# More Strassen pairs in the down projections of a two-layer decoder trunk, with wider joins and gates in its up projections

## The chip, the cores and the metric

The kernel runs on one core of a Trainium2 chip. The metric is the device time of one execution in microseconds, given as the median of several runs. All inputs lie in HBM at the start, and the output is written back there.

The engines are named as in the profile: PE is TensorE (matmuls), PEld its weight loads, DVE is VectorE, ACT is ScalarE, POOL is GpSimd, and SP is the engine whose queue issues nearly all DMAs.

## The reference

The program is a decoder trunk of two layers on 256 tokens with 1024 features. Layer 0 mixes tokens with a chunked gated MLP, layer 1 with block-sparse attention that has a relative position bias. Each layer then applies a gated feed-forward part with a causal convolution of width 3. Every part ends in a layer norm of the scaled residual sum:

```python
def conv_ffn(x, w_up, conv_w, conv_b, w_down):
    h = x @ w_up                                  # 256x1024 @ 1024x5632
    hp = jnp.pad(h, ((0, 0), (CONV_WIDTH - 1, 0), (0, 0)))
    hc = conv_b
    for j in range(CONV_WIDTH):
        hc = hc + conv_w[j] * hp[:, j:j + S]
    g, val = jnp.split(hc, 2, axis=-1)
    return (jax.nn.gelu(g) * val) @ w_down        # 256x2816 @ 2816x1024

for i in range(DEPTH):
    y = chunked_gmlp(x, ...) if i % 2 == 0 else moba_attention(x, ...)
    x = layer_norm(DN_ALPHA * x + y, ln_mix_g[i], ln_mix_b[i])
    y = conv_ffn(x, ...)
    x = layer_norm(DN_ALPHA * x + y, ln_ffn_g[i], ln_ffn_b[i])
```

All of it is float32.

## The kernel before, in words

**Numbers as two parts.** PE multiplies in the format fp32r. To keep float32 precision, each operand is split into a high part (an ACT copy to fp32r) and a low part (DVE subtracts the high part from the original). A product of two operands is then three matmuls: high by high, high by low, low by high. The function `split` (line 331) records the copy and the subtraction. Most instructions pass through a few helpers, so the profile shows them under one line each: `mms` (L300) for matmuls, `act` (L312), `tt` (L318) and `stt` (L322) for DVE, `transposes` (L306).

**Weights.** Weights come as a stream of 1 MB chunks of 128x2048. `prep` (line 445) loads one chunk into one of two `raw` buffers and splits its two halves into `whi` and `wlo` tiles of 128x1024. There are ten of each, so five chunks are ready or in work at a time: when a chunk is spent, the one five places behind it is started. The feed-forward part has 22 up chunks (`f_up0`, `f_up1`) and 11 down chunks (`f_dn0`, `f_dn1`) per layer.

**Up stage** (`conv_up`, line 850). The features run over partitions. After a first pair of tiles that is computed by rows, ten groups follow, each with two gate tiles and two value tiles. Each of the four has a PSUM bank of 512 columns: 256 hold the products with the high token part and the high weights, 256 the rest (`cols_times`). A group is 64 matmuls, half with 512 columns and half with 256. After it, `join` (line 649) adds the two halves of each bank (an ACT copy, then a DVE addition, 256 columns each), and `gate` (line 860) does for each of the two feature tiles the convolution (ACT scale and shift, DVE scalar_tensor_tensor twice, for gate and value), the gelu, the product, and the split into `rr`, all on 256 columns. The scratch tile `ff` holds what lies between.

**Down stage** (`project_out`, line 657). Tokens run over partitions, two tiles of 128. For each of 22 k tiles the two halves of 512 output columns are accumulated in four banks. A pair of k tiles is one chunk. In a normal pair there are 2 x 2 x 2 products, 24 matmuls of 128x512. The pairs listed in `FAST` are done as a Strassen product with seven products, 21 matmuls (`unit`, line 680). Four of the seven use sums of weights (`weight_forms`, line 419) and four use sums of tokens (`token_forms`, line 432), three of them both, all made by DVE and split again by ACT and DVE. The gated tokens that a fast pair needs unsplit stay in `kept` places of `ff`. Four extra banks hold the four products that are common to several outputs; they run through all fast pairs of a stage and are put together once (`combine`, line 713). After the last pair the outputs get their layer norm.

```python
FAST = {"f_dn0": (4, 7), "f_dn1": (4, 5, 7)}
```

The numbers are those of the pairs, 0 to 10, in a stage; "unit 7" below is the fast pair 7.

**What sets the order.** Every step is recorded in a `Plan` with an estimated duration, and a list scheduler then sets the order on each engine. PE follows the order of recording, except for a few filling matmuls. ACT, DVE and SP follow due times, which come from PE's estimated line. So a step that is recorded at another place, or with another estimate, moves others. Each engine then runs its list strictly in that order. `build_bias` (line 539) makes the attention's bias table; before, it is recorded between the up and down stage of layer 0.

Of the kernel before, what the change touches and what calls it, by code (L numbers as in the profile page):

```python
# [11 lines left out]
F32 = mybir.dt.float32  # L12
# [41 lines left out]
FAST = {"f_dn0": (4, 7), "f_dn1": (4, 5, 7)}  # L54
# [175 lines left out]
def trunk_kernel(ctx: ExitStack, tc: tile.TileContext, a: dict, out: bass.AP):  # L230
# [43 lines left out]
    banks = [ps.tile([P, HALF], F32, name=f"bank{i}") for i in range(BANKS)]  # L274
# [3 lines left out]
    def bank(long=False):  # L278
        i = min((i for i in range(BANKS) if not bank_of[i][2]), key=lambda i: bank_of[i][0])
# [4 lines left out]
        return b  # L284

# [6 lines left out]
    def mms(seq, r, w, fill=False, ns=None, mixed=False):  # L292

        for o, l, x, _, _ in seq if ns is None else ():
            n = flat(x)
            ns = (ns or 0.0) + max(107.0, n / 2.4) + 2.5 if l.dtype == F32R else (218.0 if n <= P else n / 0.6 + 5)
# [74 lines left out]
    def raw_of(i):  # L371
        if is_fast(i) and stream[i][1] == FAST[stream[i][0]][-1]:
            early = place("ff", 2560, CH)
        elif i == 2:
# [7 lines left out]
    raw_held, forms, kept = {}, {}, {}  # L382
    inner = {}

    def used_up(k0, k1):

        bufs = []
        for b in inner["rr"]:
            n = Buf(b.ap[:, k0 * S:k1 * S], [Buf(None)])
            n.prev[0].ops = [o for k in range(k0, k1) for o in [b.wr[k], *b.rd.get(k, ())]]  # L390
            bufs.append(n)
        return bufs
# [26 lines left out]
    def weight_forms(i):  # L419

        rb, t = raw_held[i], place("ff", 0, 4 * HALF)
        b4, t4 = (x.ap.rearrange("p (a n) -> p a n", a=4) for x in (rb, t))
        tt(t4[:, 0:2, :], b4[:, 1:4:2, :], b4[:, 0:2, :], ALU.subtract, [(rb, [*range(6), 6, 7])], [(t, [0, 1])])
        tt(t4[:, 2, :], t4[:, 1, :], b4[:, 0, :], ALU.add, [(rb, [0, 1]), (t, [1])], [(t, [2])])
        tt(t4[:, 3, :], b4[:, 2, :], t4[:, 2, :], ALU.subtract, [(rb, [4, 5]), (t, [2])], [(t, [3])])
        h, l = used_up(0, KT) if stream[i][1] in FAST[stream[i][0]][1:-1] else xt_new()
        for o in (0, 2):
            parts, sl = [o, o + 1], slice(o * HALF, (o + 2) * HALF)
            split((h, parts, h.ap[:, sl]), (l, parts, l.ap[:, sl]), (t, parts, t.ap[:, sl]))
        forms[i] = h, l  # L430

    def token_forms(key):

        g, s = kept[key], place("ff", 2048, HALF)
        a11, a21, a12, a22 = (g.ap[:, j * P:(j + 1) * P] for j in range(4))
        s1, s3, s2, s4 = (s.ap[:, j * P:(j + 1) * P] for j in range(4))
        tt(s1, a21, a22, ALU.add, [(g, [0, 1])], [(s, [0])])
        tt(s3, a11, a21, ALU.subtract, [(g, [0])], [(s, [1])])
        tt(s2, s1, a11, ALU.subtract, [(g, [0]), (s, [0])], [(s, [2])])
        tt(s4, a12, s2, ALU.subtract, [(g, [1]), (s, [2])], [(s, [3])])  # L440
        h, l = (x.new() for x in tok_rings)
        split((h, [0], h.ap), (l, [0], l.ap), (s, range(4), s.ap))
        return h, l

    def prep(i):
        name, c = stream[i]
        if i > 1 and is_fast(i - 2):
            weight_forms(i - 2)
        raw = raw_of(i)
        if name != "a_v":  # L450
# [14 lines left out]
        chunks[i], raw_held[i] = subs, raw[0][0]  # L465
# [72 lines left out]
    def build_bias(at):  # L538
        rb, oh, parts = place("ff", at, P), place("ff", at + P, DIST), xth.new()
# [117 lines left out]
    def project_out(name, nk, at, xold, li, rows_i, wait=REST, first=None):  # L657
# [22 lines left out]
        def unit(c):  # L680
# [4 lines left out]
            th, tl = forms[where[name, c]]  # L685
            sh, sl = token_forms((name, c))
# [26 lines left out]
        def combine():  # L713
# [7 lines left out]
            tt(u.ap, m6.ap, u.ap, ALU.add, [m6, u], [u])  # L721
            tt(w.ap, m5.ap, u.ap, ALU.add, [m5, u], [w])
            tt(y.ap, m7.ap, u.ap, ALU.add, [m7, u], [y])
            stt(r0.ap[:, hi], r0.ap[:, hi], ALPHA, w.ap, ALU.mult, ALU.add, [(r0, ph), w], [(r0, ph)])
            x1 = r1.ap.rearrange("p (a n) -> p a n", a=2)
            stt(x1, x1, ALPHA, y.ap.unsqueeze(1).to_broadcast([P, 2, HALF]), ALU.mult, ALU.add, [(r1, QUART), y], [(r1, QUART)])
            tt(r1.ap[:, hi], r1.ap[:, hi], m5.ap, ALU.add, [(r1, ph), m5], [(r1, ph)])
            for b in sums:
                done_with(b, 0)

        for k, t in order:
            if k // 2 in units:
# [117 lines left out]
    def conv_up(layer, h, l):  # L850
        ah, al = place("rr", 0, FT * S), place("rr", FT * S, FT * S)
        inner["rr"] = ah, al
# [3 lines left out]
        hring = Places("ff", (3456, 3712, 3968, 4224, 6 * S, 7 * S, 8 * S, 9 * S), S)  # L856
# [3 lines left out]
        def gate(i, srcs):  # L860
            cs = []
            for j, (b, o) in enumerate(srcs):
                cw, c = cc[:, layer, j * FT + i, :], cring[j].new()
                act(c.ap, o, AF.Identity, [b, convc], [c], bias=cw[:, 3:4], scale=cw[:, 2:3], psum=i < 2)
# [3 lines left out]
            key, n = (f"f_dn{layer}", i // 2), 0  # L868
            if key[1] in FAST.get(key[0], ()):
                n = i % 2  # L870
                if not n:
                    kept[key] = place("ff", 4608 + HALF * FAST[key[0]].index(key[1]), HALF)
# [271 lines left out]
```

## Time and profile before

| what | value |
|---|---|
| median of 3 runs | 557.43 us (556.71 to 557.60) |
| span of the profiled execution | 555.0 us |
| PE busy | 547.0 us, 2968 matmuls |
| DVE busy | 498.9 us |
| ACT busy | 378.3 us |
| read from HBM | 109.52 MB |
| up stage of layer 0 | to 198.79 us |
| down stage of layer 0 | 198.79 to 253.5 us |
| up stage of layer 1 | to 489.7 us |
| down stage of layer 1 | 489.7 to 547.9 us |

The span is the time from the first to the last instruction of one profiled execution. A time of the run is somewhat longer: 2.4 us lie between the span and the median. A row of a timeline has the start in us, the length, engine, line, operation, tile written and tiles read, shapes and how many instructions of the kind follow each other. A matmul's length is modelled and overlaps its neighbour; the distance between starts is what a matmul costs.

### The profile page before, as it was taken

The numbers are of one execution on the slowest core, as the hardware profiler recorded it, in microseconds if no ns is written. First come the engines' busy times: TensorE is split into PE (matmuls) and PEld (weight loads), VectorE is DVE, ScalarE is ACT, GpSimd is POOL, SyncE is SP. The second block draws the span as 40 slices with busy tenths as digits, with TensorE's granted clock in tenths as the row PEclk, the third lists the DMA queues.
The fourth block names the chain that finished last, engine by engine and source line by source line (L and its number), as shares of the span: only waits on it lengthen the run. The fifth ranks groups of instructions, "written<-read, shape, count | busy, mean of one in ns | idle before, by whom it ended". The sixth has DMA issues, their size and how long they took to land.

```text
span 555.0 us, 8220 instructions
## 1 busy us (share of the span) xinstructions
PE 547.0 (99%) x2968; PEld 468.8 (84%) x2968; DVE 498.9 (90%) x967; ACT 378.3 (68%) x718; POOL 11.3 (2%) x17
## 2 busy tenths in 40 slices
PE   9999999999999999999999999999999999999994
PEld 6888888898988988888888888888898988988884
DVE  6889889999999999989948898889898999999997
ACT  6846586877877884645668877587767877776510
POOL 0010000000000000001000000000000000000001
PEclk9999999999999999999999999999999999999998
DMA  8996626686545524764565363416765466444602
GB/s 317 413 335 238 230 92 228 227 308 224 208 172 188 191 77 153 285 227 152 191 263 191 110 251 138 174 70 233 298 232 223 155 227 227 153 151 153 220 9 76
DMA packets 20105, 111.12 MB, mean 200 GB/s; under 512 B 2256, under 2 KB 5600, under 8 KB 7904
## 3 DMA queue, kind: packets, MB, share of 16 engines
q1 hardware_dynamic: 19488, 109.94, 54.7%
q10 hardware_dynamic: 576, 0.66, 0.3%
q8 instruction: 23, 0.38, 0.3%
q14 instruction: 18, 0.15, 0.1%
HBM read 109.52 MB, written 1.07 MB: 199 GB/s over the span
## 4 chain that ended last, share of the span: by engine, by line
PE 99%; DVE 1%; issue 0%; DVEq 0%
PE bank L300 96%; PE bank L306 2%; DVE x L322 0%; DVE stat L563 0%; DVEq L1140 0%; DVE stat L569 0%
## 5 line engine op out<-in xcount | busy, mean ns | idle before, releaser
L318 DVE TENSOR_TENSOR wlo<-raw,whi 128x1024 fp32r<-128x1024 f32 (+2 forms) x205 | 216.6, 1079 | 19.9 <-ACT whi L312 13.3
L312 ACT ACTIVATE whi<-raw 128x1024 fp32r<-128x1024 f32 (+2 forms) x205 | 185.1, 941 | 61.5 <-DMA raw<-in_f_up 22.2
L300 PE MATMUL bank<-xt,whi 128*128 128x512 f32 x832 | 195.9, 391 | 0.0
L300 PEld LDWEIGHTS bank<-xt,whi 128*128 128x128 f32 x832 | 154.2, 188 | 30.6
L300 PE MATMUL bank<-whi,rr 128*128 128x512 f32 (+1 forms) x428 | 134.1, 387 | 0.0
L300 PEld LDWEIGHTS bank<-xt,wlo 128*128 128x128 f32 x832 | 103.1, 192 | 2.1
L300 PE MATMUL bank<-xt,wlo 128*128 128x256 f32 x832 | 104.8, 284 | 0.0
L300 PEld LDWEIGHTS bank<-whi,rr 128*128 128x128 f32 x428 | 80.0, 188 | 16.2 <-issue 0.2
L300 PE MATMUL bank<-wlo,rr 128*128 128x512 f32 (+1 forms) x214 | 82.6, 386 | 0.0
L322 DVE SCALAR_TENSOR_TENSOR ff<-ff,convc 128x255 f32<-128x255 f32 (+1 forms) x160 | 70.4, 476 | 0.3 <-ACT ff L312 0.2
L312 ACT ACTIVATE ff<-bank 128x256 f32<-128x256 f32 (+2 forms) x126 | 49.3, 400 | 27.1 <-PE bank L300 19.9
L300 PE MATMUL bank<-whi,xt 128*128 128x512 f32 (+1 forms) x196 | 60.7, 390 | 0.0
L318 DVE TENSOR_TENSOR ff<-bank,ff 128x256 f32<-128x256 f32 (+1 forms) x110 | 45.5, 431 | 8.5 <-ACT ff L312 7.7
L312 ACT ACTIVATE ff<-ff,convc 128x256 f32<-128x256 f32 x80 | 45.0, 592 | 3.0 <-DVE ff L318 2.9
L300 PEld LDWEIGHTS bank<-wlo,rr 128*128 128x128 f32 x214 | 40.2, 188 | 7.9
L300 PEld LDWEIGHTS bank<-whi,xt 128*128 128x128 f32 x196 | 36.4, 188 | 8.3 <-ACT whi L312 1.2
L300 PE MATMUL bank<-wlo,xt 128*128 128x512 f32 (+1 forms) x98 | 36.4, 387 | 0.0
L312 ACT ACTIVATE ff<-bank,lncol 128x128 f32<-128x128 f32 x48 | 18.7, 459 | 17.5 <-PE bank L306 17.5
L318 DVE TENSOR_TENSOR ff<-ff 128x256 f32<-128x256 f32 (+3 forms) x74 | 30.3, 431 | 0.3 <-ACT ff L312 0.2
L312 ACT ACTIVATE ff<-ff 128x256 f32<-128x256 f32 x52 | 20.4, 411 | 11.3 <-DVE rr L318 6.8
L318 DVE TENSOR_TENSOR xt<-ff,xt 128x256 fp32r<-128x256 f32 (+3 forms) x32 | 21.8, 691 | 4.1 <-ACT xt L312 4.0
L312 ACT ACTIVATE rr<-ff 128x256 fp32r<-128x256 f32 (+3 forms) x50 | 21.3, 442 | 5.2 <-DVE ff L318 5.1
(75 smaller groups left out, 360.7 us busy)
## 6 DMA issues: line engine op xcount, KB each, us to landing
raw<-in_f_up SPq DMA_DIRECT2D x44, 1024.0 KB, 4.8
raw<-in_f_dn SPq DMA_DIRECT2D x20, 1024.0 KB, 4.8
raw<-in_b_qk SPq DMA_DIRECT2D x8, 1024.0 KB, 4.9
lnrow<-in_lnrow SPq DMA_DIRECT2D x5, 1024.0 KB, 6.6
raw<-in_a_u SPq DMA_DIRECT2D x4, 1024.0 KB, 8.4
raw<-in_a_out SPq DMA_DIRECT2D x4, 1024.0 KB, 6.0
raw<-in_b_v SPq DMA_DIRECT2D x4, 1024.0 KB, 4.7
raw<-in_b_o SPq DMA_DIRECT2D x4, 1024.0 KB, 4.9
```

Of the source, the lines that this page charges most:

```text
L300: nc.tensor.matmul(o, l, x, start=start, stop=stop, skip_group_check=mixed)
L306: nc.tensor.transpose(o, x, ident.ap)
L312: plan.op("act", ns, lambda: nc.scalar.activation(o, x, func, **kw), r, w, table=table)
L318: dve(70 + 1.04 * flat(x), lambda: nc.vector.tensor_tensor(o, x, y, op=op), r, w)
L322: lambda: nc.vector.scalar_tensor_tensor(o, x, s, y, op0=op0, op1=op1), r, w)
```

## The change

1. **`FAST`**: both down stages now have four fast pairs, 3, 5, 6 and 7. Before they had two (4, 7) and three (4, 5, 7).
2. **Weight sums**: they need a whole chunk unsplit. Before they were read from the `raw` buffer. Now `load_sums` loads a second copy of the chunk, in two halves of 0.5 MB, into those places of `ff` that the up stage uses for its gates, and the sums are made there in place. The `raw` load of a fast chunk takes only the three quarters that are split as plain weights. The form is another variant of the same algorithm, with sums where there were differences. The forms of pairs 3 and 6 go to the `xt` buffer, those of 5 and 7 to the part of `rr` that the stage has used up.
3. **When they are made**: the forms of pair 3 are recorded at the start of the down stage, those of pairs 5 and 6 behind unit 3, those of pair 7 behind unit 5. Each time the copy of the chunk two places further on in the list is loaded into the places that have come free. Token sums are three DVE instructions (256, 128, 128 columns) in place of four of 128. For pairs 3 and 5 they are made in the up stage.
4. **PSUM** is one tile of 128x4096. An up group takes banks 0 to 3 or 4 to 7. One ACT copy and one DVE addition of 128x1024 join all four banks, after the whole group.
5. **Gates**: gelu, product and split now cover both feature tiles at once, 512 columns. The convolution stays at 256.
6. **`build_bias`** is recorded ahead of the first up stage and uses other buffers.
7. The planner's estimate of a matmul goes from n/2.4 + 2.5 to n/2.4 + 8 ns.
8. **`combine`** has the signs of the new variant; its number of operations stays the same.

The core of the diff:

```diff
-FAST = {"f_dn0": (4, 7), "f_dn1": (4, 5, 7)}
+FAST = {"f_dn0": (3, 5, 6, 7), "f_dn1": (3, 5, 6, 7)}
...
-    banks = [ps.tile([P, HALF], F32, name=f"bank{i}") for i in range(BANKS)]
+    psum = ps.tile([P, BANKS * HALF], F32, name="bank")
+    banks = [psum[:, i * HALF:(i + 1) * HALF] for i in range(BANKS)]
...
+    def load_sums(name, j):
+        key = name, FAST[name][j]
+        raw_sums[key] = [place("ff", o + SUB * (j % 2), SUB) for o in (0, 5 * HALF)]
+        for n, b in enumerate(raw_sums[key]):
+            load(b.ap, a[name][key[1]][:, n * SUB:(n + 1) * SUB], [(b, range(2))])
+
+    def weight_forms(name, j):
...
+        h, l = xt_new() if j % 2 == 0 else used_up(0, KT)
+        tt(f[:, b22:b12 - 1:-5, :], f[:, b12:b12 + 1, :].to_broadcast([P, 2, HALF]),
+           f[:, b22:b11 - 1 if b11 else None:-6, :], ALU.add, [(r0, [0, 1]), (r1, [1])], [(r0, [1]), (r1, [1])])
+        tt(f[:, b11, :], f[:, b22, :], f[:, b11, :], ALU.add, [(r0, [0]), (r1, [1])], [(r0, [0])])
+        tt(f[:, b21, :], f[:, b11, :], f[:, b21, :], ALU.add, [(r0, [0]), (r1, [0])], [(r1, [0])])
+        for n, raw in ((1, r1), (0, r0)):
+            parts, sl = [2 * n, 2 * n + 1], slice(n * SUB, (n + 1) * SUB)
+            split((h, parts, h.ap[:, sl]), (l, parts, l.ap[:, sl]), (raw, [0, 1], raw.ap))
+        forms[key] = h, l
+        if j + 2 < len(FAST[name]):
+            load_sums(name, j + 2)
...
+        if is_fast(i):
+            for o, n in ((0, HALF), (SUB, SUB)):
+                load(raw[0][0].ap[:, o:o + n], a[name][c][:, o:o + n], [(raw[0][0], range(o // 256, (o + n) // 256))])
...
+        def more(c):
+            for j, after in enumerate([None, KT // 2 - 1, *units[:2]]):
+                if c == after and j < len(units):
+                    weight_forms(name, j)
...
-            tiles4 = [(bank(), *sub(name, i + j // 2, j % 2)) for j in range(4)]
-            cols_times(tiles4, h, l)
+            whole, four = four_banks()
+            cols_times([(b, *sub(name, i + j // 2, j % 2)) for j, b in enumerate(four)], h, l)
...
+            c = joined.new()
+            c3, b3 = (x.rearrange("p (a n) -> p a n", a=4) for x in (c.ap, whole))
+            act(c3, b3[:, :, S:], AF.Copy, four, [c], psum=True)
+            tt(c3, b3[:, :, :S], c3, ALU.add, [*four, c], [c])
...
+            act(g.ap, gv[0].ap, AF.Gelu_apprx_tanh, [(gv[0], both)], [(g, both)], table="gelu")
+            tt(g.ap, g.ap, gv[1].ap, ALU.mult, [(g, both), (gv[1], both)], [(g, both)])
+            at = slice(i * S, (i + 2) * S)
+            split((ah, [i, i + 1], ah.ap[:, at]), (al, [i, i + 1], al.ap[:, at]), (g, both, g.ap))
+            if key in kept and key[1] in FAST[key[0]][:2]:
+                token_forms(key)
```

Three places show how the instructions move.

First, DVE late in the up stage of layer 0, before. `ff<-bank` is a join, `ff<-ff,convc` the convolution, `wlo<-raw,whi` the low part of a weight half:

```order
L318 TENSOR_TENSOR ff<-bank_112,ff 128x256
L322 SCALAR_TENSOR_TENSOR ff<-ff,convc 128x254
L318 TENSOR_TENSOR ff<-bank_105,ff 128x256
L318 TENSOR_TENSOR wlo_75<-raw_86,whi_65 128x1024
L318 TENSOR_TENSOR ff<-bank_106,ff 128x256
L318 TENSOR_TENSOR ff<-bank_107,ff 128x256
L318 TENSOR_TENSOR wlo_76<-raw_86,whi_66 128x1024
L318 TENSOR_TENSOR ff<-ff 128x256 x2
```

The joins of a group are four, each behind its own bank, with a weight half and a convolution of the tiles before in between. The same place now:

```order
L326 TENSOR_TENSOR wlo_75<-raw_86,whi_65 128x1024
L326 TENSOR_TENSOR wlo_76<-raw_86,whi_66 128x1024
L326 TENSOR_TENSOR wlo_77<-raw_85,whi_67 128x1024
L326 TENSOR_TENSOR wlo_78<-raw_85,whi_68 128x1024
L326 TENSOR_TENSOR ff<-bank,ff 128x1024
L326 TENSOR_TENSOR ff<-ff 128x512
L326 TENSOR_TENSOR small<-ff,small 128x512
```

One join stands for four, behind the weight halves; a part of the token sums of a fast pair (`small`) has come into the up stage.

Second, DVE in the down stage of layer 0 up to the weight forms of unit 7, before. These go to `xt`, and the tokens' form to `small`:

```order
L318 TENSOR_TENSOR ff<-ff 128x1024
L318 TENSOR_TENSOR wlo_78<-ff,whi_68 128x1024
L318 TENSOR_TENSOR ff<-ff 128x512
L318 TENSOR_TENSOR wlo_79<-raw_86,whi_69 128x1024
L318 TENSOR_TENSOR wlo_80<-raw_86,whi_70 128x1024
L318 TENSOR_TENSOR ff<-ff 128x512
L318 TENSOR_TENSOR wlo_77<-ff,whi_67 128x512
L318 TENSOR_TENSOR xt_87<-ff,xt_87 128x1024 x2
```

And now, where the forms of unit 6 go to `xt` and those of unit 7 to `rr`:

```order
L326 TENSOR_TENSOR xt_87<-ff,xt_87 128x1024 x2
L326 TENSOR_TENSOR small<-ff,small 128x512
L326 TENSOR_TENSOR wlo_78<-raw_86,whi_68 128x1024
L326 TENSOR_TENSOR ff<-ff 128x2x512
L326 TENSOR_TENSOR wlo_77<-raw_86,whi_67 128x512
L326 TENSOR_TENSOR ff<-ff 128x256
L326 TENSOR_TENSOR ff<-ff 128x512
L326 TENSOR_TENSOR ff<-ff 128x128
L326 TENSOR_TENSOR wlo_80<-raw_85,whi_70 128x1024
L326 TENSOR_TENSOR ff<-ff 128x128
L326 TENSOR_TENSOR wlo_79<-raw_85,whi_69 128x1024
L326 TENSOR_TENSOR ff<-ff 128x512
```

The forms of unit 7 (`rr<-ff,rr`, twice 128x1024) follow two rows behind, after the tokens' form. The weight sums of 6 and 7 stand one after the other, between the splits of chunks 7 and 8.

Third, PE in the down stage of layer 0, the second half of pair 3 before, four products of three matmuls each:

```order
L300 MATMUL bank_105<-whi_70,rr 128x512
L300 MATMUL bank_105<-wlo_80,rr 128x512
L300 MATMUL bank_105<-whi_70,rr 128x512
L300 MATMUL bank_106<-whi_70,rr 128x512
L300 MATMUL bank_106<-wlo_80,rr 128x512
L300 MATMUL bank_106<-whi_70,rr 128x512
...
L300 MATMUL bank_108<-whi_70,rr 128x512
L300 MATMUL bank_108<-wlo_80,rr 128x512
L300 MATMUL bank_108<-whi_70,rr 128x512
```

And pair 3 now, the whole unit of 21 matmuls, with the weight forms in `xt` and the token forms in `small`:

```order
L308 MATMUL bank<-whi_70,rr 128x512
L308 MATMUL bank<-wlo_80,rr 128x512
L308 MATMUL bank<-whi_70,rr 128x512
L308 MATMUL bank<-whi_70,small 128x512
L308 MATMUL bank<-wlo_80,small 128x512
L308 MATMUL bank<-whi_70,small 128x512
L308 MATMUL bank<-whi_69,rr 128x512
L308 MATMUL bank<-wlo_79,rr 128x512
L308 MATMUL bank<-whi_69,rr 128x512
L308 MATMUL bank<-xt_87,rr 128x512 x3
L308 MATMUL bank<-xt_87,small 128x512 x9
```

Nine matmuls of a unit need no weight form; the tenth is the first that reads one.

More of the change, by code (lines that the diff above doesn't have):

```diff
@@ L273, in trunk_kernel, with bank @@
     x32a, x32b = Places("ff", (4608, 5120), HALF), Places("ff", (5632, 5888), S)
-    banks = [ps.tile([P, HALF], F32, name=f"bank{i}") for i in range(BANKS)]
+    psum = ps.tile([P, BANKS * HALF], F32, name="bank")
+    banks = [psum[:, i * HALF:(i + 1) * HALF] for i in range(BANKS)]
     bank_of = [(i - BANKS, None, False) for i in range(BANKS)]
     state = {"age": 0, "next": 0, "low": False}
-    def bank(long=False):
-        i = min((i for i in range(BANKS) if not bank_of[i][2]), key=lambda i: bank_of[i][0])
+    def bank(long=False, at=None):
+        i = min((i for i in range(BANKS) if not bank_of[i][2]), key=lambda i: bank_of[i][0]) if at is None else at
         old = bank_of[i][1]
@@ L284, in bank, with four_banks @@
         return b
+    def four_banks():
+        free = [i for i in (0, 4) if not any(x[2] for x in bank_of[i:i + 4])]
+        i = min(free, key=lambda i: max(x[0] for x in bank_of[i:i + 4]))
+        return psum[:, i * HALF:(i + 4) * HALF], [bank(at=j) for j in range(i, i + 4)]
     def done_with(b, age=None):
@@ L380, in raw_of @@
         return [(early, early.ap[:, s * SUB:(s + 1) * SUB], s * 4) for s in range(2)]
-    raw_held, forms, kept = {}, {}, {}
+    forms, kept = {}, {}
     inner = {}
     def used_up(k0, k1):
+        if "spare" in inner:
+            inner["spare"] = [Buf(b.ap, [b]) for b in inner["spare"]]
+            return inner["spare"]
         bufs = []
@@ L391, in used_up @@
             bufs.append(n)
+        inner["spare"] = bufs
         return bufs
@@ L417, in is_fast @@
         return c in FAST.get(name, ())
[L419 to L440, printed above, removed]
+    raw_sums = {}
@@ L464, in prep @@
             subs.append((hi, lo))
-        chunks[i], raw_held[i] = subs, raw[0][0]
+        chunks[i] = subs
     FINE = set()
@@ L684, in unit @@
             (b11, _), (b2, _) = ((x, None) for x in (sub(name, c, 0), sub(name, c, 1)))
-            th, tl = forms[where[name, c]]
-            sh, sl = token_forms((name, c))
+            th, tl = forms[name, c]
+            if (name, c) not in tokens:
+                token_forms((name, c))
+            sh, sl = tokens[name, c]
             def token(k, t):
@@ L736, in project_out @@
                     spent(name, k // 2)
+                    more(k // 2)
                     if k // 2 == units[-1]:
@@ L743, in project_out @@
                 spent(name, k // 2)
+                if units:
+                    more(k // 2)
         res = (None, None) if last else xt_new()
@@ L867, in gate @@
                 cs.append(c)
[L868 to L872, printed above, removed]
-                g = kept[key]
-            else:
-                g = gring.new()
-            gv, gp = g.ap[:, n * S:(n + 1) * S], (g, [n])
-            act(gv, cs[0].ap, AF.Gelu_apprx_tanh, [cs[0]], [gp], table="gelu")
-            tt(gv, gv, cs[1].ap, ALU.mult, [gp, cs[1]], [gp])
-            c = slice(0, P if g is kept.get(key) and not n else S)
-            split((ah, [i], av[:, i, c]), (al, [i], lv[:, i, c]), (g, [n], gv[:, c]))
+            g = gring.new()
+            act(g.ap, cs[0].ap, AF.Gelu_apprx_tanh, [cs[0]], [g], table="gelu")
+            tt(g.ap, g.ap, cs[1].ap, ALU.mult, [g, cs[1]], [g])
+            split((ah, [i], av[:, i, :]), (al, [i], lv[:, i, :]), (g, [0], g.ap))
         turned = []
```

71 lines of the change are left out of this document (46 added, 25 removed).

## The prediction

> **What bounds the kernel now.** I read the page first, then the chain of waits, then busy time by stage, and last the timelines of PE and DVE where the change works. From the page the span and the engines' shares, then two pieces of the chain (start, length) and what ends the second:
>
> ```profile
> span 555.0 us, 8220 instructions
> ...
> PE 547.0 (99%) x2968; PEld 468.8 (84%) x2968; DVE 498.9 (90%) x967; ACT 378.3 (68%) x718; POOL 11.3 (2%) x17
> ```
> ```profile
> 89.00 164.56 PE bank L300 x876
> ...
> 379.89 167.98 PE bank L300 x902
> 547.87 0.02 issue
> ```
>
> The chain never leaves PE from 89.00 to 253.55 and from 379.89 to 547.87, which is nearly all of both up stages and all of both down stages. So the time there is the number of matmuls times their spacing, and only fewer matmuls or a new wait can move it. DVE is at 90%. Whether it has room is read stage by stage: up stage 0, down stage 0 until its last fast pair has its weights, and the same for layer 1 (columns: stretch, its length, then busy time of PE, PEld, DVE, ACT, POOL, granted clock, DMA share, GB/s):
>
> ```profile
> 90.00:198.80 108.80, 108.80 (x632) 96.62 (x631) 103.05 (x191) 84.51 (x157) 0.00 (x0) 1.00 0.58 208
> 198.80:237.00 38.20, 38.20 (x170) 31.68 (x169) 36.78 (x64) 23.17 (x36) 0.00 (x0) 1.00 0.51 192
> 380.00:489.70 109.70, 109.70 (x636) 97.32 (x635) 103.12 (x191) 86.83 (x161) 0.00 (x0) 1.00 0.61 218
> 489.70:529.20 39.50, 39.50 (x176) 32.66 (x174) 39.30 (x70) 23.98 (x35) 0.00 (x0) 1.00 0.44 160
> ```
>
> PE is busy for the whole of each, at a granted clock of 1.00. DVE idles 5.75, 1.42, 6.58 and 0.20 us. That is nearly all the room there is for more Strassen pairs, whose forms DVE must make.
>
> **Fewer matmuls.** The timeline of PE in down stage 0, inside the fast pair 4, and its first row:
>
> ```profile
> 198.79 0.39 PE L300 MATMUL bank<-whi,rr 128*128 128x512 f32 x1
> ...
> 223.47 2.20 PE L300 MATMUL bank<-xt,small 128*128 128x512 f32 x9
> 225.51 0.39 PE L300 MATMUL bank<-whi,rr 128*128 128x512 f32 x1
> ```
>
> Nine matmuls of 128x512 take 225.51 - 223.47 = 2.04 us from start to start, 0.2267 us each. A normal pair of k tiles is 8 products of 3 matmuls, 5.44 us. A fast pair is 7 products, 4.76 us. Fast pairs go from 2 to 4 in down stage 0 and from 3 to 4 in down stage 1. That is three more, nine matmuls fewer, **2.04 us** (1.36 and 0.68). All of it is on the chain. [...]
>
> **What DVE pays for a fast pair.** Where DVE's time could end up on PE is unit 7, the last fast pair of both stages. These rows show it before the change: DVE's splits of its weight forms, then PE's matmuls that read them, first of down stage 0, then of down stage 1:
>
> ```profile
> 233.44 2.36 DVE L318 TENSOR_TENSOR xt<-ff,xt 128x1024 fp32r<-128x1024 f32 x2
> 235.71 2.36 DVE L318 TENSOR_TENSOR wlo<-raw,whi 128x1024 fp32r<-128x1024 f32 x2
> ```
> ```profile
> 238.43 0.84 PE L300 MATMUL bank<-xt,rr 128*128 128x512 f32 x3
> 239.11 2.20 PE L300 MATMUL bank<-xt,small 128*128 128x512 f32 x9
> ```
> ```profile
> 526.88 2.35 DVE L318 TENSOR_TENSOR xt<-ff,xt 128x1024 fp32r<-128x1024 f32 x2
> 529.15 4.62 DVE L318 TENSOR_TENSOR wlo<-raw,whi 128x1024 fp32r<-128x1024 f32 x4
> ```
> ```profile
> 528.44 0.84 PE L300 MATMUL bank<-xt,rr 128*128 128x512 f32 x3
> 529.12 2.26 PE L300 MATMUL bank<-xt,small 128*128 128x512 f32 x9
> 531.22 0.39 PE L300 MATMUL bank<-whi,rr 128*128 128x512 f32 x1
> ```
>
> The prices come from the groups of DVE instructions by shape (busy time, mean ns of one, idle before):
>
> ```profile
> L318 DVE TENSOR_TENSOR wlo<-raw,whi 128x1024 fp32r<-128x1024 f32 x153 | 183.3, 1217 | 16.6 <-ACT whi L312 10.1 <-PE bank L300 4.5 <-ACT ff L312 1.2
> L318 DVE TENSOR_TENSOR ff<-bank,ff 128x256 f32<-128x256 f32 x104 | 41.6, 417 | 8.4 <-ACT ff L312 7.7
> L322 DVE SCALAR_TENSOR_TENSOR ff<-ff,convc 128x255 f32<-128x255 f32 x80 | 36.7, 476 | 0.2 <-ACT ff L312 0.2
> L318 DVE TENSOR_TENSOR wlo<-raw,whi 128x512 fp32r<-128x512 f32 x50 | 32.5, 681 | 2.9 <-ACT whi L312 2.8
> L318 DVE TENSOR_TENSOR ff<-ff 128x256 f32<-128x256 f32 x44 | 17.4, 417 | 0.2 <-ACT ff L312 0.2
> L318 DVE TENSOR_TENSOR rr<-ff,rr 128x256 fp32r<-128x256 f32 x39 | 15.1, 417 | 0.0
> L318 DVE TENSOR_TENSOR xt<-ff,xt 128x1024 fp32r<-128x1024 f32 x8 | 9.4, 1218 | 0.0
> L318 DVE TENSOR_TENSOR ff<-ff 128x512 f32<-128x512 f32 x8 | 5.5, 684 | 0.1
> L318 DVE TENSOR_TENSOR ff<-ff 128x128 f32<-128x128 f32 x20 | 5.2, 282 | 0.0
> L318 DVE TENSOR_TENSOR small<-ff,small 128x512 fp32r<-128x512 f32 x5 | 3.4, 687 | 0.5 <-ACT small L312 0.5
> ```
>
> Neighbours overlap. Above, two of 1218 ns begin 2.27 us (235.71 - 233.44) ahead of the next row, 1.135 each, so in a run of instructions each costs 0.08 less than its mean: 1.135, 0.60, 0.34 and 0.20 us for 1024, 512, 256 and 128 columns. A fast pair of the new kernel has one weight sum and two splits of 1024 (3.41), two weight sums and the token split of 512 (1.80), and token sums of 256, 128 and 128 (0.74). It saves half the split of its chunk's first half (0.54). Sum 5.41 us, within 0.1 of the old form. The sum over a 128x2x512 view with a broadcast operand is in no row; I price it as 1024 columns, with half and twice that as ends (-0.6, +1.1 us a pair).
>
> **What the up stage gives back.** Four joins of 256 become one of 1024 (1.36 to 1.135), two products of 256 one of 512 (0.68 to 0.60), two splits likewise: 0.38 us a group, 3.8 us over ten groups. The eight scalar_tensor_tensor rows per group stay as they are. [...]
>
> So DVE's extra work is 2 x 5.41 - 3.8 = 7.0 us in layer 0 and 5.41 - 3.8 = 1.6 us in layer 1. It must be done before unit 7's forms are read, since the added pairs 3, 5 and 6 all lie ahead of unit 7.
>
> In stage 0 the last form ends at 235.8 and PE wants it at 239.11: 3.3 us to spare. In stage 1 it ends at about 529.2, just where PE wants it, and nine matmuls there take 2.10 us and not 2.04. Unit 7 already touches its limit in layer 1.
>
> The budget: layer 0 has 5.75 + 1.42 of idle, and 3.3 - 1.36 to spare, since PE will be 1.36 earlier. That is 9.1 us of room for 7.0 of work, 2.1 left. Layer 1 has 6.58 + 0.20 + 0 - 0.68 = 6.1 for 1.6, 4.5 left. By the order of the new kernel, DVE runs from the last group's join to unit 7's second form through 19 instructions of 1024, 15 of 512, eight of 0.40 (scalar_tensor_tensor), two of 256 and four of 128: 21.6 + 9.0 + 3.2 + 0.7 + 0.8 = 35.3 us. The join needs ACT's copy of 1024 columns out of PSUM first, about 1 us by four times the row of 256 less its overlap:
>
> ```profile
> L312 ACT ACTIVATE ff<-bank 128x256 f32<-128x256 f32 x104 | 38.7, 376 | 25.0 <-PE bank L300 19.9 <-DVE ff L322 1.6 <-ACT whi L312 0.8
> ```
>
> Started 1.3 us after the up stage's last matmul, it ends at +36.6. PE reaches that form after 3 normal pairs, unit 3, pair 4, units 5 and 6, and 12 matmuls of unit 7: 16.32 + 4.76 + 5.44 + 9.52 + 2.72 = +38.8. So 2.2 us to spare if DVE is on time and idles nowhere. Units 3, 5 and 6 have more. The cover is thin, and what lies over 2.2 us goes on PE in full.
>
> **Edits with one answer.** Second weight copies: 0.75 MB more per fast pair, 6 MB in all, on queues whose DMA share was 0.51 and 0.44 in the down stages above. A whole chunk lands in
>
> ```profile
> raw<-in_f_dn SPq DMA_DIRECT2D x20, 1024.0 KB, 4.8
> ```
>
> The copies for units 6 and 7 are sent when pairs 3 and 5 have left their buffers, some 3 us ahead of DVE's use; two halves of a chunk take between half of that row, 2.4, and all of it. I take no cost, because DVE has other splits queued there; at worst it is 1.8 us of DVE idle for each, which is rival one. The new wait, a join behind four finished banks, holds up on ACT the weight copies queued behind the PSUM copy, and on DVE the gates; both are wanted only a group, 11 us, later, and PE needs the four banks again after that long. The position bias, moved ahead of the first up stage, is one matmul either way. The combination of the sums has the same count. The tail behind 547.87 (7.1 us of the span) is the same. The new spacing in the planner's estimate only reorders.
>
> **The sum.** The profiled span is 555.0, the median 557.43: 2.4 us lie around it, and I keep them. 555.0 - 2.04 = 553.0, and 557.43 - 2.04 = **555.4 us**. A measurement of this kernel can tell 0.2%, 1.1 us, so the gain is visible only if at most 0.9 us of it is lost.
>
> **Rivals.** First, *unit 7 waits a little* (chance 0.22). Idle of the old kind stays in part: in up stages DVE waited for ACT like this (total us, times, longest; layer 0, then layer 1):
>
> ```profile
> DVE ff L318 <- ACT ff L312: 2.7, 7, 0.7
> ```
> ```profile
> DVE wlo L318 <- ACT whi L312: 4.1, 3, 2.1
> ```
>
> If about 3.5 of the 7.2 us of idle in layer 0 remain, unit 7 is 3.5 - 2.1 = 1.4 us late, and 557.43 - 2.04 + 1.4 = 556.8: no visible change. For it: the second stage already loses 0.06. Against: a DVE that is behind finds its inputs ready, and joins that wait for ACT fall from four to one a group.
>
> Second, *slower* (0.14): the join of four banks starts only when all four are done and ACT has copied 1024 columns, where before three of the four had been joined during the group. DVE then idles about as much as before in both up stages, every group. It is behind at the end of both, and units 5 to 7 wait: layer 0 loses 7.2 - 2.1 = 5.1, layer 1 6.8 - 4.5 = 2.3, and the time is 557.43 - 2.04 + 7.4 = 562.8. It turns slower than before once 2.04 is lost, so from about 4.1 us of idle left in layer 0 alone, 0.4 us a group; visibly from 5.2. For it: DVE is in order, and nothing behind the join can pass it. Against: there are four weight splits of 1.135 us per group, and the order has one to four of them right ahead of each join. [...]
>
> Third, *the change doesn't remove matmuls, or gives the 2 us back elsewhere*, as in a LayerNorm stage that now waits (0.04): 557.4.
>
> **How the numbers follow.** No visible stall (0.60): 555.0 to 556.3. Rival one: 556.3 to 557.6. Rival two from 558.5 to 562.8. The range that leaves out most of rival two and the odd low run (medians scatter by 0.4) is 554.9 to 557.5. Faster by over 0.2%: 0.60 and a part of rival one, 0.65. Within: 0.20. Slower: 0.15.
>
> **What would show it.** Nine fewer 128x512 matmuls and a span near 553.0, PE busy throughout 198 to 253 and the last stage, with DVE idle in the up stages down to some 2 us per layer: right. Idle before the first `xt` or `rr` weight matmul of unit 7: rival one. DVE idle of 5 us in the up stages and PE waiting in units 5, 6 and 7: rival two. A PE wait within an up group would break the view that banks come free in time.

## The result, and the profile after

The change makes the kernel slower. The median after is 563.19 us (six runs, 562.29 to 569.39), beside 557.57 for the kernel before on the same chip (556.71 to 557.73): a ratio of 1.0128, 95% interval 1.0085 to 1.0171. The forecast was 555.4, in 554.9 to 557.5. The runs after also scatter over 7 us, those of before over 1.

From the page of after, the span and the engines' shares:

```profile
span 567.7 us, 8102 instructions
...
PE 553.3 (97%) x2959; PEld 470.8 (83%) x2959; DVE 509.2 (90%) x891; ACT 374.8 (66%) x627; POOL 11.8 (2%) x17
```

The matmuls are 2968 - 2959 = 9 fewer, as announced. But PE now idles 567.7 - 553.3 = 14.4 us, where before it idled 8.0. (This is the profile of the run at 569.39, the slowest of the six.) The critical path, which was PE throughout both down stages, now has this in it, by engine and by line:

```profile
PE 78%; DVE 9%; DMA 8%; issue 3%; ACT 2%; SPq 0%; DVEq 0%; ACTq 0%
PE bank L308 75%; DMA ff<-in_f_dn 5%; DVE ff L326 4%; PE bank L314 2%; DMA raw<-in_f_dn 2%; DVE wlo L326 2%; DVE ff L330 1%; DVE rr L326 1%; ACT whi L320 1%; DMA raw<-in_head 1%; ACT xt L320 0%; DVE x L330 0%; DVE xt L326 0%; ACT rr L320 0%; DVE small L326 0%
```

`ff<-in_f_dn` is the second weight copies: 5% of the span waits for them to land. By stage, the same four stretches as before (stretch, length, busy time of PE, PEld, DVE, ACT, POOL, granted clock, DMA share, GB/s):

```profile
93.60:202.40 108.80, 108.80 (x632) 96.57 (x631) 106.42 (x165) 82.65 (x114) 0.00 (x0) 1.00 0.58 215
202.40:240.60 38.20, 37.23 (x165) 30.50 (x163) 33.67 (x47) 19.64 (x25) 0.00 (x0) 1.00 0.65 214
387.10:496.80 109.70, 109.70 (x635) 97.31 (x634) 107.12 (x165) 85.37 (x119) 0.00 (x0) 1.00 0.60 215
496.80:536.30 39.50, 36.66 (x162) 30.03 (x160) 33.76 (x47) 19.75 (x25) 0.00 (x0) 0.99 0.61 206
```

The up stages are as long as before, PE never stops in them, and DVE idles 2.4 and 2.6 us there. In the down stages DVE idles 38.20 - 33.67 = 4.5 and 39.50 - 33.76 = 5.7 us, where it idled 1.4 and 0.2, and the DMA share went from 0.51 and 0.44 to 0.65 and 0.61. What DVE waits for stands in the waits (total us, times, longest):

```profile
DVE ff L326 <- DMA ff<-in_f_dn: 8.4, 7, 2.5
```

How that reaches PE is read in the last down stage. First the chain of waits (start, length):

```profile
511.15 7.00 DMA ff<-in_f_dn
...
518.25 3.25 DVE ff L326 x5
...
524.98 5.04 DMA ff<-in_f_dn
...
530.11 1.23 DVE ff L326
...
535.55 0.60 DVE ff L326
536.15 0.61 DVE rr L326
...
536.81 8.38 PE bank L308 x24
```

Halves of the chunks land 7.00 and 5.04 us after they are sent, and PE stands at the end. DVE's own rows for that stretch, with its idle time in brackets:

```profile
510.40 0.68 DVE L326 TENSOR_TENSOR rr<-ff,rr 128x512 fp32r<-128x512 f32 x1
...
514.52 1.23 DVE L326 TENSOR_TENSOR ff<-ff 128x1024 f32<-128x1024 f32 x1 [1.10 <-DMA ff<-in_f_dn]
518.25 4.04 DVE L326 TENSOR_TENSOR ff<-ff 128x1024 f32<-128x1024 f32 x7 [2.50 <-DMA ff<-in_f_dn]
...
530.11 1.23 DVE L326 TENSOR_TENSOR ff<-ff 128x1024 f32<-128x1024 f32 x1 [1.15 <-DMA ff<-in_f_dn]
```

DVE stands at the first weight sums of units 6, 5 and 7, in this order, 4.75 us in all. Everything behind those rows in its list is late by that, the plain splits too, which need no copy. The longest wait, 2.50 us, is for the second half of unit 5's copy: it goes into a place of the up stage's gates and could be sent, at 511.15, only when DVE had split the last of them (the row at 510.40). PE's rows at the first product of unit 7, in the same stage:

```profile
532.85 0.39 PE L308 MATMUL bank<-whi,rr 128*128 128x512 f32 x1
533.08 0.39 PE L308 MATMUL bank<-wlo,rr 128*128 128x512 f32 x1
536.81 0.80 PE L308 MATMUL bank<-whi,rr 128*128 128x512 f32 x1 [3.35 <-DVE rr L326]
...
538.68 0.63 PE L308 MATMUL bank<-whi,rr 128*128 128x512 f32 x1
539.11 0.63 PE L308 MATMUL bank<-wlo,rr 128*128 128x512 f32 x1
...
543.89 0.39 PE L308 MATMUL bank<-whi,rr 128*128 128x512 f32 x1
544.12 0.39 PE L308 MATMUL bank<-wlo,rr 128*128 128x512 f32 x1
```

PE waits 3.35 us, not yet for a weight form but for the low part of unit 7's tokens, which DVE makes just ahead of the forms. After it the matmuls start 0.43 us apart (538.68, 539.11), until they are 0.23 apart again at 543.89. The first down stage has the same spacing, after two shorter waits:

```profile
240.24 0.50 PE L308 MATMUL bank<-whi,small 128*128 128x512 f32 x1 [0.97 <-ACT small L320]
...
241.85 0.61 PE L308 MATMUL bank<-whi,small 128*128 128x512 f32 x1 [0.89 <-DVE small L326]
242.25 0.63 PE L308 MATMUL bank<-whi,rr 128*128 128x512 f32 x1
242.68 0.63 PE L308 MATMUL bank<-wlo,rr 128*128 128x512 f32 x1
```

In these two stretches the granted clock is 0.50, and 1.00 between them:

```profile
242.10:245.50 3.40, 3.40 (x8) 2.20 (x8) 3.40 (x4) 2.73 (x5) 0.00 (x0) 0.50 0.73 289
245.50:535.65 290.15, 287.96 (x1610) 245.44 (x1608) 260.70 (x501) 202.54 (x367) 4.36 (x4) 1.00 0.56 198
535.65:542.45 6.80, 5.64 (x13) 4.46 (x14) 6.80 (x8) 5.06 (x6) 0.00 (x0) 0.50 0.53 175
```

PE is busy for 3.40 and 5.64 us of them, and nearly half of that is lost to the clock, some 4 us in this execution (0.43 us a matmul in place of 0.23); in the last stage the wait is paid nearly twice. The second of the two stretches begins at 535.65, a little over 2 us into the wait that ends at 536.81, and the first at 242.10, after waits of 0.97 and 0.89 us. In another execution (e1 below) waits of 0.88 and 0.85 us in the first stage, and of 3.06 and 0.77 us in the last, left the clock at 1.00.

### The profile page after: what moved, and what is told of

Read it like the earlier page. It is cut to its first block, busy times and chain, and to the rows that moved or that the text cites. A ratio compares the mean times of both kernels' runs of the same rounds, so it can differ in the third digit from the quotient of the medians.

```text
span 567.7 us, 8102 instructions
## 1 busy us (share of the span) xinstructions
PE 553.3 (97%) x2959; PEld 470.8 (83%) x2959; DVE 509.2 (90%) x891; ACT 374.8 (66%) x627; POOL 11.8 (2%) x17
## 4 chain that ended last, share of the span: by engine, by line
PE 78%; DVE 9%; DMA 8%; issue 3%; ACT 2%; SPq 0%; DVEq 0%; ACTq 0%
PE bank L308 75%; DMA ff<-in_f_dn 5%; DVE ff L326 4%; PE bank L314 2%; DMA raw<-in_f_dn 2%; DVE wlo L326 2%; DVE ff L330 1%; DVE rr L326 1%; ACT whi L320 1%; DMA raw<-in_head 1%; ACT xt L320 0%; DVE x L330 0%; DVE xt L326 0%; ACT rr L320 0%; DVE small L326 0%
## 5 line engine op out<-in xcount | busy, mean ns | idle before, releaser
L308 PE MATMUL bank<-whi,rr 128*128 128x512 f32 (+1 forms) x392 | 125.5, 391 | 3.3 <-DVE rr L326 3.3
L308 PEld LDWEIGHTS bank<-whi,rr 128*128 128x128 f32 x392 | 73.6, 189 | 18.9 <-DVE rr L326 4.0
L308 PE MATMUL bank<-wlo,rr 128*128 128x512 f32 (+1 forms) x196 | 76.0, 388 | 0.0
L330 DVE SCALAR_TENSOR_TENSOR ff<-ff,convc 128x255 f32<-128x255 f32 (+1 forms) x160 | 67.1, 478 | 0.1
L326 DVE TENSOR_TENSOR ff<-ff 128x512 f32<-128x512 f32 (+3 forms) x76 | 45.0, 615 | 8.4 <-DMA ff<-in_f_dn 8.4
L320 ACT ACTIVATE ff<-bank 128x256 f32<-128x256 f32 (+3 forms) x66 | 39.6, 617 | 19.3 <-PE bank L308 19.0
L326 DVE TENSOR_TENSOR ff<-bank,ff 128x256 f32<-128x256 f32 (+2 forms) x50 | 37.5, 769 | 1.8 <-ACT ff L320 1.8
L320 ACT ACTIVATE rr<-ff 128x512 fp32r<-128x512 f32 (+2 forms) x36 | 24.5, 692 | 15.7 <-DVE ff L326 15.7
L326 DVE TENSOR_TENSOR rr<-ff,rr 128x512 fp32r<-128x512 f32 (+2 forms) x36 | 27.4, 773 | 1.4 <-ACT rr L320 1.4
L326 DVE TENSOR_TENSOR xt<-ff,xt 128x256 fp32r<-128x256 f32 (+2 forms) x31 | 21.6, 702 | 2.3 <-ACT xt L320 2.0
```

The lines of the kernel that those rows point to most:

```text
L308: nc.tensor.matmul(o, l, x, start=start, stop=stop, skip_group_check=mixed)
L320: plan.op("act", ns, lambda: nc.scalar.activation(o, x, func, **kw), r, w, table=table)
L326: dve(70 + 1.04 * flat(x), lambda: nc.vector.tensor_tensor(o, x, y, op=op), r, w)
L330: lambda: nc.vector.scalar_tensor_tensor(o, x, s, y, op0=op0, op1=op1), r, w)
```

## The experiments

The theory (A): the second weight copies land late, DVE stands in front of them, and units 5 to 7 wait. Rivals: (B) the wide joins or DVE's extra work make DVE late whatever the copies do; (C) it is the new order of the instructions, and not the bytes; (D) the loss is mostly the clock after the wait. Each kernel was timed against the kernel before on its chip (557.2 to 557.5).

**e1, the changed kernel again**, for the spread.

> The changed kernel unchanged, for a second profile. Theory A (late copies): DVE stands at the weight sums because the second copies of the fast chunks land 5 to 7 us after they are sent, so unit 7 is late in both down stages. It expects 562 to 564 us and again 3 to 5 us of DVE waiting for copies in each down stage, with PE waits only in units 5 to 7. Theory B (DVE overloaded by the four-bank joins) expects DVE to be behind already at the end of each up stage, by over 2 us. Theory C (chance: the first loads and the clock) expects the profile's late start of 2.4 us to come back.

Measured 566.19 us (563.99 to 567.0), ratio 1.0153 (1.0133 to 1.0173). Its profile is of the fastest of these runs, and shows DVE and PE waiting again, at a granted clock of 1.00 in both down stages. The theory had 562 to 564 us:

```profile
DVE ff L326 <- DMA ff<-in_f_dn: 7.6, 7, 2.1
PE bank L308 <- DVE rr L326: 4.7, 3, 3.1
```

**e2, no copies.** The sums are made of what lies in the buffers, and the planner orders anew:

```diff
-        for n, b in enumerate(raw_sums[key]):
-            load(b.ap, a[name][key[1]][:, n * SUB:(n + 1) * SUB], [(b, range(2))])
+        for b in raw_sums[key]:
+            last = max((o for q in b.prev for o in q.ops), key=lambda o: o.i)
+            b.wr = {0: last, 1: last}
```

> The second copies are left out: the weight sums are made of whatever lies in those places, so they are not the weights' sums; every other instruction is there. A: no wait for copies, unit 7 on time, about 555.4 us (555 to 556.5). B: the DVE work is the same, so 561 to 564 us. C: as the changed kernel, 561 to 564.

Measured 556.60, 0.9990 (0.9981 to 0.9998): 9.6 us under e1, with PE waiting for no engine in any stage of its profile. DVE has all its sums and all joins, so B falls. C is open, since the order is another.

**e3 and e6, the old pairs** in the new kernel, with copies and without:

```diff
-FAST = {"f_dn0": (3, 5, 6, 7), "f_dn1": (3, 5, 6, 7)}
+FAST = {"f_dn0": (4, 7), "f_dn1": (4, 5, 7)}
```

> The changed kernel with the old lists of pairs (4, 7 and 4, 5, 7): new joins, gates, copies, but nine more matmuls and three pairs' forms fewer. A: layer 0 has more than a stage of time for its two copies and layer 1 is in between: 557 to 559 us. B: the up stages are as in the changed kernel and DVE has 10.8 us less in layer 0, but in layer 1 only 5.4 less: 557 to 561, with DVE behind at the end of the up stages.

> The old lists of pairs and no second copies (the sums are of other data): only the new joins, gates and the moved position bias remain against the kernel before. The changed kernel with the old pairs took 560.1. A2 says that its loss was the copies in SP's queue: 557 to 558.2. If the wide joins and gates cost time by themselves, it stays at 559 to 560.

Measured 560.11, 1.0060 (1.0038 to 1.0083), and 558.32, 1.0018 (1.0009 to 1.0027). Five pairs lose 1.8 us to their copies, eight lose 9.6 (by the medians, each kernel in an order of its own). And e6 against e2 is what three more pairs bring without copies: 1.7 us of the 2.04.

**e8, no copies and the old estimate** of a matmul:

```diff
-            ns = (ns or 0.0) + max(107.0, n / 2.4 + 8.0) if l.dtype == F32R else (218.0 if n <= P else n / 0.6 + 5)
+            ns = (ns or 0.0) + max(107.0, n / 2.4) + 2.5 if l.dtype == F32R else (218.0 if n <= P else n / 0.6 + 5)
```

> No second copies, and the planner's old estimate of a matmul. Without copies the kernel took 556.6, 1.2 us above the prediction's sum. If the new estimate shifts fills and layer-norm steps for the worse, this gives 555.4 to 556; if not, 556.6 or more.

Measured 565.89, 1.0157 (1.0144 to 1.0170). This was the surprise: the same instructions as in e2, 9.3 us more, only by their order, and again PE stands before a split of DVE:

```profile
PE bank L308 <- DVE rr L326: 6.2, 3, 3.4
```

So an order alone can cost as much as the copies. C had to be tested at equal order.

**e14 and e13, the order of the changed kernel held fixed.** e14 plans the copies but sends none. e13 sends each at its place, with 8 of its 1024 columns (4 KB for 512), and the planner takes it for a whole one:

```diff
-            load(b.ap, a[name][key[1]][:, n * SUB:(n + 1) * SUB], [(b, range(2))])
+            load(b.ap[:, :8], a[name][key[1]][:, n * SUB:n * SUB + 8], [(b, range(2))], nbytes=P * SUB * 4)
```

> The same order again, with no second copy sent at all (the sums are of other data), so no wait for one. The earlier kernel without copies had an order of its own. If waiting for copies is the whole loss against 556.6, this gives 556 to 557.5. If the order itself is poor too, 558 to 561.

> Every engine runs the changed kernel's list in the same order, but each second copy moves 8 of its 1024 columns (the sums are then mostly of other data). The moment of sending, SP's order and every wait stay; only the 8 MB go. If the bytes and the queue behind them make copies late: 556 to 558. If the late sending and the fixed part of a load do it: 561 to 566, near the unchanged kernel.

Measured 557.12, 1.0001 (0.9992 to 1.0009), and 556.98, 0.9996 (0.9988 to 1.0005). With every instruction at the place where e1 has it, the loss is gone, whether the small copies are sent or nothing is. It is the size of the copies: not their being sent, not the order, not DVE's work. The down stages of e13:

```profile
200.50:238.70 38.20, 38.20 (x170) 31.61 (x170) 38.17 (x52) 22.73 (x28) 0.00 (x0) 1.00 0.47 153
...
492.20:531.70 39.50, 39.50 (x176) 32.69 (x175) 39.50 (x53) 24.30 (x31) 0.00 (x0) 1.00 0.42 141
```

PE is busy throughout, DVE idles 0.03 us in the first and nowhere in the second. The landing times (KB each, median us from issue to landing) of e13:

```profile
raw<-in_f_dn SPq DMA_DIRECT2D x8, 512.0 KB, 3.7
raw<-in_f_dn SPq DMA_DIRECT2D x8, 256.0 KB, 3.9
ff<-in_f_dn SPq DMA_DIRECT2D x16, 4.0 KB, 1.6
```

and of e1:

```profile
ff<-in_f_dn SPq DMA_DIRECT2D x16, 512.0 KB, 4.3
raw<-in_f_dn SPq DMA_DIRECT2D x8, 512.0 KB, 4.6
raw<-in_f_dn SPq DMA_DIRECT2D x8, 256.0 KB, 5.3
```

A small copy is there in 1.6 us, a whole one in 4.3 in the median, and beside it the `raw` loads of the fast pairs land later: 3.7 to 4.6 and 3.9 to 5.3. Those of the other pairs, 1 MB each, do not: 5.1 in e13 and 4.8 in e1.

**e16, e4, e12, the copies planned later.** The planner counts 2, 3 or 5 us more from the sending of a copy to its use, so it puts other work of DVE ahead of the sums. e15 is e4's order with no copy sent.

```diff
+COPY = 3000.0
...
-                o.end = bus
+                o.end = bus + COPY * (o.nbytes % 2)
...
-            load(b.ap, a[name][key[1]][:, n * SUB:(n + 1) * SUB], [(b, range(2))])
+            load(b.ap, a[name][key[1]][:, n * SUB:(n + 1) * SUB], [(b, range(2))], nbytes=P * SUB * 4 + 1)
```

> With copies, the planner told of 2 us more instead of 3 (559.9) or 5 (562.3). If the later landing is a matter of how much: between the changed kernel and 559.9, 560 to 563. If each order is good or bad for other reasons, anywhere from 557 to 566.

> The planner is told that a second copy lands 3 us later than it assumed (its own load model is below the measured 4.7 us), and so puts other DVE work ahead of the sums; the work is the same. A: most of the waits for copies go, 556 to 560 us. B and C: no change, 561 to 564.

> As with the planner told of copies 3 us later, but 5 us. Copies land 5 to 7 us after they are sent, where the planner's own model has 2.4. If its order is the cause and 3 us was still too little: 556.5 to 559. If the copies' hold on SP's queue is the rest: 559 to 561.

> The order made for copies 3 us later (559.9 with copies), with no copy sent. If what was left there were waits for copies: 556 to 557.5. If that order costs time by itself: 558 to 560.

Measured, in this order, 562.31 (1.0093, 1.0075 to 1.0112), 559.93 (1.0042, 1.0026 to 1.0057), 562.34 (1.0090, 1.0068 to 1.0111) and, without copies, 556.78 (0.9990, 0.9979 to 1.0001). The middle delay takes back two thirds of e1's loss, the shorter and the longer one less; 5 us lies outside both of its forecasts. With any of the three, DVE's list of waits has no copy left. With 3 us, unit 7 is still held up a little:

```profile
PE bank L309 <- DVE rr L327: 1.6, 2, 0.9
PE bank L309 <- DVE small L327: 0.9, 1, 0.9
```

That the sums come later is not the reason: e15 has the same order and loses nothing. At this order the bytes cost 559.93 - 556.78 = 3.1 us, and they do so by another way, the `raw` loads. ACT stands in front of those, and the high parts of unit 7's forms are behind them in ACT's list. The last stage, ACT, first in e4, then in e15:

```profile
527.51 1.06 ACT L321 ACTIVATE whi<-raw 128x1024 fp32r<-128x1024 f32 x1 [5.05 <-DMA raw<-in_f_dn]
```
```profile
520.89 1.06 ACT L321 ACTIVATE whi<-raw 128x1024 fp32r<-128x1024 f32 x1 [3.06 <-DMA raw<-in_f_dn]
```

The load behind the 5.05 us was sent at 520.65 and landed 6.78 us later; the same load took 4.69 us in e15. How much of the loss of the changed kernel goes this way, and how much by DVE's own waits, was not separated.

**e7 and e5, the copies on other queues**, ACT's and POOL's, with 4.5 us planned for each:

```diff
-            load(b.ap, a[name][key[1]][:, n * SUB:(n + 1) * SUB], [(b, range(2))])
+            src = a[name][key[1]][:, n * SUB:(n + 1) * SUB]
+            plan.op("act", 60.0, lambda b=b, src=src: nc.scalar.dma_start(b.ap, src), (), [(b, range(2))], nbytes=1)
```

> The same with the copies sent by ACT's queue: ACT runs strictly in order, so it stands until the place is free, but the raw loads on SP are free of the copies. A2: 556 to 559. A1 alone: about 560. If ACT's standing matters, above 560.

> The second copies are sent by GpSimd's own queue, and the planner counts 4.5 us for each. Theory A (late copies) has two parts by now: A1, the planner's order has DVE stand at the sums before a copy lands; A2, the copies wait in SP's queue for their places and hold up the raw loads behind them (and are held up by them). Telling the planner alone gave 559.9. If A2 holds, this is another 2 to 4 us faster: 556 to 558. If only A1 holds, about 560.

Measured 563.37, 1.0107 (1.0074 to 1.0139), and 576.67, 1.0362 (1.0341 to 1.0384). On ACT's queue a copy takes the same 4.3 us:

```profile
ff<-in_f_dn ACTq DMA_DIRECT2D x16, 512.0 KB, 4.3
```

So SP's queue as such is not what makes a copy late. The POOL version tells little: there the planner takes the two halves one after the other, so all sums come much later, which is another order.

**e9, the wait filled** with products of zeros ahead of unit 7 in both stages, some 3 us each:

```diff
+            if c == 7:
+                mms([(c11.ap, zeros[0], zeros[1], False, False)] * 4, [], [c11], ns=1.0)
```

> The changed kernel with four float32 matmuls of zeros (128x512, some 3.4 us of PE time) put ahead of unit 7 in both down stages, so that PE works where it waited; 6.8 us of work more. Theory D (the clock falls after the wait and each matmul of unit 7 then takes 0.43 instead of 0.227 us): PE's wait is filled and the clock stays up, so the time stays at 563 to 567 or falls, by up to 3 us a stage, in spite of the added work. Against D (the slow matmuls are waits for operands and not a clock): the wait is filled, nothing else changes, 564 to 570, and the slow spacing in unit 7 stays.

Measured 566.23, 1.0158 (1.0135 to 1.0181): 6.1 us more work for PE, and the time of e1 (566.19). The first down stage, PE:

```profile
236.54 3.61 PE L308 MATMUL bank<-const-float32-0.0 128*128 128x512 f32 x8
239.59 0.80 PE L308 MATMUL bank<-whi,rr 128*128 128x512 f32 x1
240.22 0.39 PE L308 MATMUL bank<-wlo,rr 128*128 128x512 f32 x1
```

The filling lies where the wait was: in this profile PE waits no more ahead of unit 7 in the first stage, and 0.77 us in the last. The granted clocks on record bear on D. In all four runs of e9 the mean over the run is 0.997 or 0.998. Of the ten runs of the changed kernel (six of the result, four of e1) the four with 0.996 or more took 562.3 to 564.0 us, the six with less 562.7 to 569.4. So D is not most of the loss: e1's profiled run, with the clock at 1.00 in both down stages, is 6.8 us slower than before. A fallen clock comes on top in some executions, some 4 us in the one of the result above.

**e10 and e11, the kernel before** with a third pair in layer 0, (4, 5, 7), and with the new estimate of a matmul.

> The kernel before with pair 5 added in the first down stage (4, 5, 7 in both). No second copies: the sums read the raw buffer. DVE has 6 us more in layer 0 where it had 9.1 us of room. If room of DVE is what counts: 0.68 us less, 556.5 to 557. If the thin order of its work counts, unit 7 waits and it is 558 to 561.

> The kernel before with the planner's new estimate of a matmul (n/2.4 + 8 ns). Without copies the old estimate made the new kernel 9.3 us slower. If the estimate closer to the measured 0.227 us gives the better order in general: 556 to 557.5. If it only suits the order of the new kernel: 558 to 562.

Measured 560.33, 1.0047 (1.0030 to 1.0063), and 560.11, 1.0046 (1.0030 to 1.0063). Three matmuls fewer cost the old kernel 2.8 us, so its order did not bear this third pair. Under the new estimate the old kernel no longer computes the same values, for a reason that was not traced, so that time is only a hint.

**e17 and e18, one load for pairs 6 and 7.** Their chunks are loaded once, into the places of the copies, and the plain weight parts are split from there ahead of the sums; 3 MB less are read. e18 adds the 3 us of e4.

```diff
+    def once(i):
+        subs = []
+        for b, n, parts in zip(raw_sums[stream[i]], (HALF, SUB), ([0], [0, 1])):
+            hi, lo = whi.new(), wlo.new()
+            split((hi, range(n // 256), hi.ap[:, :n]), (lo, range(n // 256), lo.ap[:, :n]), (b, parts, b.ap[:, :n]))
+            subs.append((hi, lo))
+        chunks[i] = subs
```

> Pairs 6 and 7 are loaded once: the copy in the up-stage buffer also serves for their plain splits, and their raw loads (0.75 MB each) are gone; 3 MB less in all, the whole computation is done. If bytes in the queues make the copies late, this takes a part of the loss away: 558 to 562, with less than 8 us of DVE waiting for copies. If only the moment of sending counts: 563 to 566.

> The same, and the planner told that a copy lands 3 us later, which alone gave 559.9. Both together, if they add: 556.5 to 558.5, near the copyless 556.8. If the order is luck: anywhere to 563.

Measured 560.53, 1.0062 (1.0047 to 1.0076), and 557.75, 1.0010 (1.0000 to 1.0019). With both, the whole computation with four fast pairs is as fast as before, and 8.4 us faster than e1. PE's waits in e18, all of them (the first is at the start of the program):

```profile
PE bank L309 <- PEq L1206: 0.8, 1, 0.8
PE bank L309 <- DVE rr L327: 0.8, 1, 0.8
```

No version that computes everything beat the kernel before.

## Why the prediction was wrong

**Matmuls, right.** Nine fewer, and where DVE is on time they bring their share: from the first matmul of the down stage to the end of its products takes 59.6 us before and 58.0 in e2 in layer 0 (two pairs and the bias matmul, 1.36 + 0.2), and from the first to the end of the last matmul 58.2 and 57.4 in layer 1 (one pair, 0.68).

**DVE's prices and the hand sum, right.** The sum forecast unit 7's second form 36.6 us after the up stage. In e13, with the copies out of the way, the two forms are the first row here:

```profile
234.78 2.35 DVE L326 TENSOR_TENSOR rr<-ff,rr 128x1024 fp32r<-128x1024 f32 x2
237.05 2.36 DVE L326 TENSOR_TENSOR wlo<-raw,whi 128x1024 fp32r<-128x1024 f32 x2
```

The stage's first matmul is at 200.5, and the second form ends at 237.1: 36.6. The sum over 128x2x512, which no row showed, was priced as 1024 columns and costs 1218 ns in e13, as much as a split.

**Up stages, right.** Equal length, DVE idle of 2.4 and 2.6 us for the forecast "some 2 us", no wait within a group. Rival two, the slower one, had the sign and nearly the size (562.8), but its mechanism did not happen; that its number came near is luck.

**The step that failed** is under the edits with one answer: "I take no cost, because DVE has other splits queued there; at worst it is 1.8 us of DVE idle for each, which is rival one." Four things in it were wrong. The landing time: 2.4 to 4.8 us were allowed, by a row of 1 MB loads; the copies are sent with other copies and with the `raw` loads of two chunks around them, and land after 4.7 us in the median and after 7.0 at worst. "Some 3 us ahead of DVE's use" was on the safe side: the halves that DVE waited for in the last stage were sent 4.0 to 4.6 us before it wanted them. DVE still stands 0.4 to 2.5 us at each of three copies, 3.2 us in the first stage and 4.75 in the last. The number: only the copies for units 6 and 7 were counted, and the longest wait is for unit 5's. The other splits: they stand behind the sum in DVE's list, and DVE doesn't pass: in the last stage ACT had made the high parts of three of them by 527.82, and DVE, idle for 1.15 us up to 530.11, began them at 531.25, 532.99 and 534.33. And the bound was never set against the cover: two copies at 1.8 are 3.6 us against a cover of 2.2. That would have been 1.4 us late in a stage.

In the changed kernel, layer 0, the forms come here:

```profile
241.72 2.35 DVE L326 TENSOR_TENSOR rr<-ff,rr 128x1024 fp32r<-128x1024 f32 x2
```

They end at 244.07, 41.7 us after the first matmul at 202.4: 5.1 late against a cover of 2.2. About 3 are left; in this execution they are the PE waits of 0.97 and 0.89 us and the slowed matmuls shown above. Rival one had this place, but at 1.4 us.

Of the 9.2 us between the medians of e1 and e13, the profiles explain 1.5 in the first down stage (where e13 has a wait of its own, see below) and 4.4 in the last, 5.9 in all; but e1's profile is of its fastest run, 2.2 us under its median, and e13's of its slowest, 1.6 over. The other three runs of e1, at 565.4 to 567.0, have a mean granted clock of 0.992 to 0.994, the profiled one 0.997. So a part of the rest is likely the clock; how much is not shown.

**"The new spacing in the planner's estimate only reorders" failed** as well: reordering is not free in a kernel whose DVE has 2 us to spare (e8, 9.3 us; e16, e4 and e12, 2.4 us apart with the same work). Without copies the new estimate alone is worth those 9.3 us.

**Still open.** The copyless kernels stand at 556.6 to 557.1 and not at 555.4. By their profiles, some 0.7 to 0.9 us is lost ahead of the first down stage (0.2 of it the bias matmul that was moved there) and 0.5 to 1.2 between it and the second up stage; in e13, PE waits 1.2 us for DVE at a layer norm:

```profile
PE bank L314 <- DVE x L333: 1.2, 1, 1.2
```

e6, which has the old number of matmuls, is 1.1 slower than before without any copy, so this part belongs to the rest of the change. Which edit of it was not tried. And in the one profile of after another 2.4 us lie in a first load that came late, which no other profile has.

## What to carry to other kernels

A load that an engine in strict order waits for is priced from its sending to its landing (for 512 KB here 4.7 us in the median and 7.0 at worst), behind all that is sent with it, and against the time that the order gives it; what stands behind that instruction pays too, whether it needs the load or not (here for 4.75 us in the last stage). The bytes can also delay other loads, and the engine that waits for those: with the copies ACT stood 5.05 us for a `raw` load, without them 3.06 (e4 and e15). A worst case that is written down must be set against the cover in the same sum: here 3.6 against 2.2 us was on the page. In a list-scheduled kernel that is full on two engines, an experiment that changes the work also changes the order, which was worth 9.3 us in e8; hold the order fixed (send a few bytes in place of many) before a cause is named.

## What the hardware showed beyond that

A load of 4 KB landed in 1.6 us (e13), one of 512 KB in 4.3 to 4.7 in the median with others under way (e1 and the kernel of the result). Other 512 KB loads on SP's queue took 3.7 us in the median beside copies of 4 KB and 4.6 beside whole ones.

A PE wait of 3.35 us cost nearly as much again by a granted clock of 0.50, while waits of 3.06 and 0.77 us in another execution cost only themselves. The length of a wait alone does not decide it: the clock also fell after waits of 0.97 and 0.89 us, and stayed up after 0.88 and 0.85. What decides it is not shown here. The runs of the changed kernel scatter from 562.3 to 569.4 us.
